# Fourteen instead of twelve column pairs per MLP multiplied with seven products, and the up projection dealt out anew between them

## The chip, the cores and the metric

The kernel runs on one core of a Trainium2 chip. The metric is the time of one execution on the device in microseconds (us); the time before is the median of three runs. The engines are named as in the profile: PE does the matmuls, DVE and ACT the elementwise work, POOL issues the accumulating DMAs, SP all other loads of weights. Each engine takes its instructions in the order in which the program holds them.

## What is computed

A trunk of two layers on 256 tokens of width 2048 in float32. Each layer adds a mixer (attention and a state space model in layer 0, dilated attention in layer 1) and then an MLP to the residual x. The change is in the MLP alone, which both layers have:

```python
def squared_relu_mlp(h, w_up, w_down):
    u = jnp.einsum('bsd,df->bsf', h, w_up)
    return jnp.einsum('bsf,fd->bsd', jnp.square(jax.nn.relu(u)), w_down)

for layer in range(DEPTH):
    h = rms_norm(x, norm_mix[layer])
    x = x + mixer(h)
    h = rms_norm(x, norm_ffn[layer])
    x = x + squared_relu_mlp(h, w_up[layer], w_down[layer])
```

w_up is 2048 x 8192 and w_down 8192 x 2048.

## The kernel before

Every product is made of three matmuls, since each float32 operand is split into a high part and a remainder (high x high, high x low, low x high). The weights are split as they come: ACT rounds a loaded piece to whi (`high`, L314), DVE subtracts it to get wlo (`low`, L324). A **piece** is two contraction tiles of 128 rows by 512 columns, 512 KB of weights.

The work is one list, `plan`, of pieces, and `run` (L291) goes through it. For piece i it records, in this order, the low part of piece i+2, the load of piece i+6, the high part of piece i+3, the sum of weights for piece i+4 (`add`, if it has one), the evictions of the piece before, then some steps of side work (`tick`), and then the piece's matmuls. So this list sets the order on all engines, and DVE and ACT work a few pieces ahead of PE, as far as the buffers go: four wraw, five whi, four wlo (L303, L320, L327).

There are two kinds of work in the list:

- A `Unit` (L227) is one stripe of 512 columns. A piece of it is 12 matmuls: two contraction tiles, two halves of 128 tokens, three matmuls each. It accumulates in two PSUM tiles `acc`. `up(i)` (L1006) makes block i (of 16) of the up projection in eight pieces; `down(c, j)` (L1012) adds chunk c's part of stripe j in four pieces. A chunk is two blocks of the up projection, 1024 rows of w_down; there are eight chunks.
- A `Seven` (L245) takes two stripes by two halves of the tokens by two blocks, that is a product of 2 x 2 with 2 x 2 blocks, and does it with seven products instead of eight. Each product has two pieces of six matmuls (tile `sp`), 14 pieces in all, in the order P1, P2, Q6, Q7, Q5, Q4, Q3. The products need sums of operands: `operands(c)` (L974) makes those of the activations on DVE, once a chunk. Sums of weight blocks are made in two ways: DVE adds them (`add`, L265: for Q6 and Q4), and POOL issues a DMA that adds a block from memory onto one that is loaded (`accumulate`, L271: after the splits of P1 and P2). Q6 needs the sum of P1's accumulated block, Q7 takes P2's accumulated block directly. The tile of all these weights is `sraw`, in a pool of 29 buffers. After each product DVE adds it into the residual `res` (`evict`, L283).

In a layer the first 16 up pieces come alone; then seven sections follow, one per chunk 0 to 6. A section lays the pieces of that chunk's sevens between a number of up pieces (`mixed`, L1036); the numbers are 20, 20, 8, 20, 20, 24 and 0 (L1049). Chunks 0, 1, 3, 4 and 5 have both of their pairs of stripes as sevens; chunk 2 has the pair 0 and 1, chunk 6 the pair 2 and 3, and their other stripes are down units. Chunk 7 is four down units, put in the last section.

Side work is held in generators that `tick` moves on, one or a few steps a piece: `squared` (relu, eight transposes `uT` on PE, squares on ACT into `uf`) and `operands` (the split of `uf` into uh and ul, then the sums s, split into sh and sl). Where a piece needs a result that the side work has not recorded yet, `need` (L189) records the steps at once. Chunk 7's `operands` waits until block 15 is squared before it splits blocks 14 and 15.

When a stripe of the residual is complete, the norm of the next layer begins on it (`Norm.begin`, L490): transposes, scaling and split into hThi and hTlo, and the sum of squares. In layer 1 the stripe is stored instead (`store`, L1118). Before, this hung on chunk 7's down unit of the stripe, which was the last to add to it.

Of the kernel before, what the change touches and what calls it, by code (L numbers as in the profile page):

```python
# [20 lines left out]
W = 512  # L21
KC = 2
NS = D // W
# [17 lines left out]
def trunk(ctx: ExitStack, tc: tile.TileContext, x, norm_mix, norm_ffn, w_up, w_down, ab_w_in, ab_q_norm,  # L41
# [107 lines left out]
    done = set()  # L149
# [95 lines left out]
    class Seven:  # L245


        def __init__(self, w, rows, c0, kts, operands, to, needs, mark):
            self.w, self.rows, self.c0, self.operands, self.to, self.needs, self.mark = \
                w, rows, c0, operands, to, needs, mark  # L250
            self.halves = kts // KC
            self.raw, self.bank = {}, {}
            self.pieces = [(self, (p, h)) for p in range(7) for h in range(self.halves)]
# [29 lines left out]
        def evict(self, p):  # L283

            name, b, _ = SEVEN[p]
            t, j, op = {"P1": (0, 0, OP.add), "P2": (0, 0, OP.add), "Q6": (1, 0, OP.add), "Q7": (1, 1, OP.subtract),
                        "Q5": (1, 1, OP.subtract), "Q4": (1, 0, OP.add), "Q3": (0, 1, OP.subtract)}[name]
            r = self.to[t][j]
            V.tensor_tensor(r, r, self.bank[b], op=op)

    def run():  # L291
        todo = plan
# [328 lines left out]
                last(t, j)  # L621
        free(ps)

    def residual_unit(w, ktiles, j, needs={}, nm=None, last=None, check=None, mark=None):
        def after(ps):
            if check is not None:
                check()
            add_stripe(ps, j, last)
            if nm is not None:
                nm.begin(j)  # L630

        return Unit([(w, j * W, W)], ktiles, after, needs=needs, mark=mark)
# [316 lines left out]
    NC = NB // 2  # L949

    def mlp(layer, nm, nxt, last=None):
        wu, wd = w_up[layer], w_down[layer]
        uf, u, sums = {}, {}, {}
# [19 lines left out]

        def operands(c):  # L974

            for k in marks[c - 1] if 0 < c < NC - 2 else [("up", layer)] if c else []:
                yield from until(k)
            if c == NC - 1:
                yield from until(("uf", layer, 2 * c + 1))
            for i in (2 * c, 2 * c + 1):  # L980
                yield from until(("uf", layer, i))
                u[i] = slot("uh"), slot("ul")
                split(u[i][0], u[i][1], uf[i])
                done.add(("u", layer, i))
# [12 lines left out]
            for (h, l), s in zip(sums[c], (s1, s2)):  # L997
                split(h, l, s)
                yield 1
# [12 lines left out]
        def down(c, j):  # L1012
            kts = [(4 * (2 * c + b) + k, (lambda b=b, k=k: u[2 * c + b] + (k,))) for b in range(2) for k in range(4)]
            marks[c].append(("down", layer, c, j))
            if c < NC - 1:
                return residual_unit(wd, kts, j, {4 * b: ("u", layer, 2 * c + b) for b in range(2)},
                                     mark=marks[c][-1]).pieces

            def whole():
                assert all(("down", layer, k, j) in done or ("down", layer, k, j - j % 2) in done for k in range(NC - 1))  # L1020

            return residual_unit(wd, kts, j, {4 * b: ("u", layer, 2 * c + b) for b in range(2)}, nxt, last, whole).pieces

        def seven(c, j):
            def parts(name):
# [5 lines left out]
            return Seven(wd, (8 * c, 8 * c + 4), j * W, 4, parts,  # L1031
                         [[res[:, t, (j + i) * W:(j + i + 1) * W] for i in range(2)] for t in range(2)],
                         {0: ("u", layer, 2 * c), 1: ("u", layer, 2 * c + 1), 2: ("sums", layer, c)},
                         marks[c][-1]).pieces

        def mixed(rest, s, start, end):  # L1036

# [8 lines left out]
        ups = sum((up(i) for i in range(NB)), [])  # L1046
        plan.extend(ups[:16])
        o = 16
        for c, n in enumerate((20, 20, 8, 20, 20, 24, 0)):  # L1049
            x, o = ups[o:o + n], o + n  # L1050
            if c == NC - 2:
                x = sum((down(c, j) for j in (0, 1)), []) + sum((down(c + 1, j) for j in range(NS)), [])
                mixed(x, seven(c, 2), 2, 19)
            elif n == 8:
                mixed(x + down(c, 2) + down(c, 3), seven(c, 0), 4.5, 16)
            else:
                mixed(x, seven(c, 0) + seven(c, 2), 4.5, n + (3 if n == 24 else 0))

    n2 = Norm(R_MIX + 16, False)
    mlp(0, n1, n2)  # L1060
# [111 lines left out]
```

## Time and profile before

| | |
|---|---|
| time, median of 3 runs (lowest to highest) | 2263.64 us (2263.55 to 2264.37) |
| the profiled execution's own time | 2264.74 us |
| its span, first to last instruction | 2262.9 us |
| DMA traffic | 475.10 MB, mean 210 GB/s |
| granted TensorE clock over the span | 1.000 |

A row of the groups reads: source line, engine, operation, output tile <- input tiles, shapes, count, then busy us and mean ns of one, then the idle time before them and what ended it. A row of the timeline or of the chain begins with the start in us from the first instruction and the duration. A row of the waits has total us, times, longest. A row of the windows has the stretch, its length, the busy us of PE, weight loads, DVE, ACT and POOL, the granted clock, the share of the DMA engines and GB/s. Nearly all instructions carry L71, the line of a helper, so tiles tell them apart: `acc` is a unit's matmul and `sp` a seven's; wlo<-wraw is the split of a unit's piece and wlo<-sraw that of a seven's.

### The profile page before, as it was taken

How to read it: one execution, taken by the hardware profiler on the slowest of the kernel's cores; microseconds unless marked ns; L12 is line 12 of the kernel's file. 1: busy time of each engine (PE TensorE's matmuls, PEld its weight loads, DVE VectorE, ACT ScalarE, POOL GpSimd, SP SyncE). 2: the span in 40 equal slices, each digit the busy share in tenths (PEclk: the TensorE clock that was granted, in tenths of full speed). 3: DMA queues.
4: the chain of work that ended last, by engine and by line, in shares of the span. 5: the costliest groups of instructions: out<-in, count | busy, mean ns of one | idle time of the engine just before them, and what ended most of it. 6: DMA issues, size and time to landing. Idle time of an engine off the chain costs nothing.

```text
span 2262.9 us, 30235 instructions
## 1 busy us (share of the span) xinstructions
PE 2247.2 (99%) x11029; PEld 1873.0 (83%) x11029; DVE 1749.7 (77%) x2482; ACT 1290.0 (57%) x1615; POOL 125.7 (6%) x116
## 2 busy tenths in 40 slices
PE   8999999999999999999999999999999999999999
PEld 7998988888888888888788778778888888888877
DVE  6779986556888888887976766665588888888786
ACT  6565545445666556565664555555566665656663
POOL 1000000000001010000000000000000000010000
PEclk9999999999999999999999999999999999999999
DMA  7546555568797797888756455546788789797874
GB/s 235 163 142 190 177 177 182 190 186 246 216 296 214 209 288 222 242 245 234 219 171 192 149 158 168 168 151 186 245 237 240 206 242 281 207 282 228 248 222 141
DMA packets 255318, 475.10 MB, mean 210 GB/s; under 512 B 17156, under 2 KB 27696, under 8 KB 255168
## 3 DMA queue, kind: packets, MB, share of 16 engines
q1 hardware_dynamic: 218976, 416.34, 56.7%
q0 software_dynamic: 26624, 50.48, 12.5%
q10 hardware_dynamic: 9568, 6.34, 0.9%
q8 instruction: 86, 1.41, 0.2%
q14 instruction: 64, 0.52, 0.1%
HBM read 470.97 MB, written 2.13 MB: 209 GB/s over the span
## 4 chain that ended last, share of the span: by engine, by line
PE 97%; DMA 1%; DVE 1%; issue 1%; ACT 0%; SPq 0%; DVEq 0%; POOLq 0%; ACTq 0%
PE acc L71 71%; PE sp L71 20%; PE uT L71 1%; PE sc L71 1%; PE o L71 1%; DMA sraw<-in_w_down_dram 1%; PE pT L71 1%; PE yp L71 1%; PE xT L71 1%; DVE wlo L71 1%; DMA wraw<-in_ab_w_in_dram 0%; PE qp L71 0%; DMA res<-in_x_dram 0%; PE yo L71 0%; PE kp L71 0%
## 5 line engine op out<-in xcount | busy, mean ns | idle before, releaser
L71 ACT ACTIVATE whi<-wraw 128x1024 fp32r<-128x1024 f32 (+1 forms) x600 | 631.9, 1054 | 493.6 <-PE acc L71 350.8
L71 DVE TENSOR_TENSOR wlo<-wraw,whi 128x1024 fp32r<-128x1024 f32 (+1 forms) x600 | 725.0, 1214 | 233.7 <-PE acc L71 159.7
L71 PE MATMUL acc<-whi,hThi 128*128 128x512 f32 (+1 forms) x1632 | 647.7, 397 | 1.8 <-ACT hThi L71 1.7
L71 PE MATMUL acc<-whi,hTlo 128*128 128x512 f32 (+1 forms) x1632 | 634.8, 389 | 1.0 <-DVE hTlo L71 1.0
L71 PE MATMUL acc<-wlo,hThi 128*128 128x512 f32 (+1 forms) x1632 | 634.1, 389 | 0.7 <-DVE wlo L71 0.7
L71 ACT ACTIVATE whi<-sraw 128x1024 fp32r<-128x1024 f32 x336 | 353.7, 1059 | 292.4 <-DVE sraw L71 137.0
L71 DVE TENSOR_TENSOR wlo<-sraw,whi 128x1024 fp32r<-128x1024 f32 x336 | 408.8, 1221 | 85.3 <-PE acc L71 35.3
L71 PEld LDWEIGHTS acc<-whi,hThi 128*128 128x128 f32 x1632 | 307.6, 188 | 66.8 <-issue 5.8
L71 PEld LDWEIGHTS acc<-whi,hTlo 128*128 128x128 f32 x1632 | 307.2, 188 | 65.7 <-DVE hTlo L71 1.8
L71 PEld LDWEIGHTS acc<-wlo,hThi 128*128 128x128 f32 x1632 | 307.9, 189 | 60.9 <-DVE wlo L71 1.1
L276 POOL DMA_DIRECT2D sraw<-in_w_down_dram x96 | 117.3, 1576 | 2058.7 <-DVE wlo L71 1815.6
L71 PE MATMUL sp<-wlo,sh 128*128 128x512 f32 x384 | 149.5, 389 | 0.0
L71 PE MATMUL sp<-whi,sl 128*128 128x512 f32 x384 | 149.5, 389 | 0.0
L71 PE MATMUL sp<-whi,sh 128*128 128x512 f32 x384 | 149.4, 389 | 0.0
L71 DVE TENSOR_TENSOR sraw<-sraw 128x1024 f32<-128x1024 f32 x96 | 117.1, 1219 | 26.4 <-DMA sraw<-in_w_down_dram 26.3
L71 DVE TENSOR_TENSOR res<-res,sp 128x512 f32<-128x512 f32 x168 | 114.7, 682 | 17.4 <-PE sp L71 17.1
L71 PE MATMUL acc<-hThi,whi 128*128 128x256 f32 x384 | 112.3, 293 | 0.0
L71 PE MATMUL sp<-whi,ul 128*128 128x512 f32 x288 | 112.1, 389 | 0.0
L71 PE MATMUL sp<-whi,uh 128*128 128x512 f32 x288 | 112.0, 389 | 0.0
L71 PE MATMUL sp<-wlo,uh 128*128 128x512 f32 x288 | 112.0, 389 | 0.0
L71 PE MATMUL acc<-hThi,wlo 128*128 128x256 f32 x384 | 108.5, 283 | 0.0
L71 PE MATMUL acc<-hTlo,whi 128*128 128x256 f32 x384 | 108.5, 283 | 0.0
(221 smaller groups left out, 2749.8 us busy)
## 6 DMA issues: line engine op xcount, KB each, us to landing
wraw<-in_w_up_dram SPq DMA_DIRECT2D x256, 512.0 KB, 5.2
sraw<-in_w_down_dram SPq DMA_DIRECT2D x192, 512.0 KB, 8.1
wraw<-in_ab_w_in_dram SPq DMA_DIRECT2D x96, 512.0 KB, 3.7
sraw<-in_w_down_dram POOLq DMA_DIRECT2D x96, 512.0 KB, 10.7
wraw<-in_c_w_qkv_dram SPq DMA_DIRECT2D x96, 512.0 KB, 4.2
wraw<-in_w_down_dram SPq DMA_DIRECT2D x64, 512.0 KB, 4.2
wraw<-in_ab_w_out_dram SPq DMA_DIRECT2D x48, 512.0 KB, 3.7
wraw<-in_c_w_o_dram SPq DMA_DIRECT2D x32, 512.0 KB, 3.6
```

The lines of the kernel that those rows point to most:

```text
L71: return f(out, *a, **k)
L276: nc.gpsimd.dma_start(self.raw[o[0], h], self.w[r * 128:(r + KC) * 128, c:c + W].rearrange("(k p) c -> p k c", p=128), accum_op=OP.add)
```

## The change

Chunks 2 and 6 take both pairs of stripes as sevens, so 14 of the 16 pairs of a layer do; only chunk 7 is left in down units. The sections' up pieces are now 18, 17, 17, 18, 17, 17 and 8: the last up unit stands in the last section, ahead of chunk 7's down units. Since a stripe's last addition may now come from chunk 6's seven or from chunk 7's down unit, a count per stripe (`early`) finds the second of the two, and the norm or the store follows that. `operands(6)` waits for chunk 5's sevens as the other chunks do for theirs, and no longer for the last up unit.

```diff
@@ class Seven
-        def __init__(self, w, rows, c0, kts, operands, to, needs, mark):
+        def __init__(self, w, rows, c0, kts, operands, to, needs, mark, after=None):
...
             V.tensor_tensor(r, r, self.bank[b], op=op)
+            if p == 6 and self.after is not None:
+                self.after()
@@ def operands(c)
-            for k in marks[c - 1] if 0 < c < NC - 2 else [("up", layer)] if c else []:
+            for k in marks[c - 1] if 0 < c < NC - 1 else [("up", layer)] if c else []:
@@ def down(c, j)
-            def whole():
-                assert all(("down", layer, k, j) in done or ("down", layer, k, j - j % 2) in done for k in range(NC - 1))
-
-            return residual_unit(wd, kts, j, {4 * b: ("u", layer, 2 * c + b) for b in range(2)}, nxt, last, whole).pieces
+            def after(ps):
+                if early[j]:
+                    add_stripe(ps, j, last)
+                else:
+                    add_stripe(ps, j)
+                early[j] += 1
+                ready(j, False)
+
+            return Unit([(wd, j * W, W)], kts, after,
+                        needs={4 * b: ("u", layer, 2 * c + b) for b in range(2)}).pieces
+
+        early = [0] * NS
+
+        def ready(j, stored=True):
+
+            if early[j] == 2:
+                if last is not None and stored:
+                    for t in range(2):
+                        last(t, j)
+                if nxt is not None:
+                    nxt.begin(j)
+
+        def sevens_end(j):
+            for k in (j, j + 1):
+                early[k] += 1
+                ready(k)
...
-                         marks[c][-1]).pieces
+                         marks[c][-1], (lambda: sevens_end(j)) if c == NC - 2 else None).pieces
@@ the list
-        for c, n in enumerate((20, 20, 8, 20, 20, 24, 0)):
+        for c, n in enumerate((18, 17, 17, 18, 17, 17, 8)):
             x, o = ups[o:o + n], o + n
+            s = seven(c, 0) + seven(c, 2)
             if c == NC - 2:
-                x = sum((down(c, j) for j in (0, 1)), []) + sum((down(c + 1, j) for j in range(NS)), [])
-                mixed(x, seven(c, 2), 2, 19)
-            elif n == 8:
-                mixed(x + down(c, 2) + down(c, 3), seven(c, 0), 4.5, 16)
+                mixed(x + sum((down(c + 1, j) for j in range(NS)), []), s, 4, 23)
             else:
-                mixed(x, seven(c, 0) + seven(c, 2), 4.5, n + (3 if n == 24 else 0))
+                mixed(x, s, 4.5, n)
```

Two places in the order of instructions are needed later. The first is DVE at the start of chunk 1's first seven in the first MLP, before the change. wlo<-sraw is the split of a seven's piece, wlo<-wraw that of an up piece, so these rows also tell in which order the pieces stand; sraw<-sraw is a sum of weights, res<-res,sp the addition of a finished product.

```order
L71 TENSOR_TENSOR wlo<-wraw,whi 128x1024
L71 TENSOR_TENSOR wlo<-sraw,whi 128x1024 x2
L71 TENSOR_TENSOR wlo<-wraw,whi 128x1024
L71 TENSOR_TENSOR sraw<-sraw 128x1024
L71 TENSOR_TENSOR wlo<-sraw,whi 128x1024
L71 TENSOR_TENSOR res<-res,sp 128x512
L71 TENSOR_TENSOR wlo<-sraw,whi 128x1024
L71 TENSOR_TENSOR sraw<-sraw 128x1024
L71 TENSOR_TENSOR wlo<-wraw,whi 128x1024
L71 TENSOR_TENSOR wlo<-sraw,whi 128x1024
```

And DVE at the same place with the change, from the split of the seven's second piece on:

```order
L71 TENSOR_TENSOR wlo<-sraw,whi 128x1024
L71 TENSOR_TENSOR wlo<-wraw,whi 128x1024
L71 TENSOR_TENSOR wlo<-sraw,whi 128x1024 x2
L71 TENSOR_TENSOR sraw<-sraw 128x1024
L71 TENSOR_TENSOR res<-res,sp 128x512
L71 TENSOR_TENSOR wlo<-wraw,whi 128x1024
L71 TENSOR_TENSOR sraw<-sraw 128x1024
L71 TENSOR_TENSOR wlo<-sraw,whi 128x1024 x2
L71 TENSOR_TENSOR res<-res,sp 128x512
L71 TENSOR_TENSOR wlo<-wraw,whi 128x1024
L71 TENSOR_TENSOR wlo<-sraw,whi 128x1024 x2
```

The seven's pieces stand in pairs with one up piece between them, where before there was an up piece after the first and then after every second; and the second sum of weights stands ahead of the split of the first sum (the first row after it), where it stood behind it.

The second place is ACT at the end of the first MLP's up projection. Before the change, at chunk 6's first down piece, the split of block 12 (uh) stands behind the weight splits (whi), with the relu of block 15 behind it:

```order
L71 ACTIVATE whi<-sraw 128x1024
L71 ACTIVATE whi<-wraw 128x1024
L71 ACTIVATE uh<-uf 128x1024
L71 ACTIVATE relu<-acc,rs_4976 128x512 x2
L71 ACTIVATE uh<-uf 128x1024
L71 ACTIVATE whi<-wraw 128x1024
```

With the change, at chunk 7's first down piece, for the splits of blocks 14 and 15:

```order
L71 ACTIVATE whi<-sraw 128x1024 x2
L71 ACTIVATE whi<-wraw 128x1024
L71 ACTIVATE relu<-acc,rs_4976 128x512 x2
L71 ACTIVATE uf<-uT 128x512 x2
L71 ACTIVATE uh<-uf 128x1024 x2
L71 ACTIVATE whi<-sraw 128x1024
```

The two relu and the two squares (uf) of block 15, with PE's eight transposes (uT) between them, now stand ahead of the split that the down piece waits for.

More of the change, by code (lines that the diff above doesn't have):

```diff
@@ L245, in trunk @@
     class Seven:
-        def __init__(self, w, rows, c0, kts, operands, to, needs, mark):
-            self.w, self.rows, self.c0, self.operands, self.to, self.needs, self.mark = \
-                w, rows, c0, operands, to, needs, mark
+        def __init__(self, w, rows, c0, kts, operands, to, needs, mark, after=None):
+            self.w, self.rows, self.c0, self.operands, self.to, self.needs, self.mark, self.after = \
+                w, rows, c0, operands, to, needs, mark, after
             self.halves = kts // KC
@@ L622, in add_stripe, with residual_unit @@
         free(ps)
-    def residual_unit(w, ktiles, j, needs={}, nm=None, last=None, check=None, mark=None):
+    def residual_unit(w, ktiles, j, needs={}, nm=None, last=None, mark=None):
         def after(ps):
-            if check is not None:
-                check()
             add_stripe(ps, j, last)
```

## The prediction, made before the changed kernel was run

> **What bounds the kernel now.** I read the page first: which engine is full, and what the chain that ended last is made of.
>
> ```profile
> PE 2247.2 (99%) x11029; PEld 1873.0 (83%) x11029; DVE 1749.7 (77%) x2482; ACT 1290.0 (57%) x1615; POOL 125.7 (6%) x116
> PE 97%; DMA 1%; DVE 1%; issue 1%; ACT 0%; SPq 0%; DVEq 0%; POOLq 0%; ACTq 0%
> ```
>
> PE is the bound: 99% busy, and 97% of the chain is PE. So a matmul that goes is time that goes, as long as PE is not made to wait. What a matmul costs on the path is not its own duration (0.39 us in the timeline, where they overlap) but the step from one to the next. The chain in order of time shows it, here in the output projection and then in the first MLP's chunk 1:
>
> ```profile
> 394.31 29.95 PE acc L71 x132
> ...
> 641.65 1.36 PE sp L71 x6
> 643.02 0.44 PE uT L71 x4
> 643.45 2.75 PE acc L71 x12
> 646.21 2.72 PE sp L71 x12
> ...
> 660.28 2.72 PE acc L71 x12
> ```
>
> 29.95 us for 132 is **0.227 us a matmul**. A piece of an ordinary unit (U below, 12 matmuls) takes 2.72 us, a piece of a seven (S, 6 matmuls) 1.36 us. I number a seven's 14 pieces S0 to S13: S0, S1 are P1, S2, S3 P2, S4, S5 Q6, S6, S7 Q7, S8, S9 Q5, S10, S11 Q4, S12, S13 Q3. Every piece, U or S, needs one split by ACT and DVE, so an S asks twice as much of DVE per microsecond of PE. How near that is to the edge shows over a whole chunk (chunk 4 of the first MLP, 20 U and 28 S), in which DVE is busy 80.94 of 94.38 us and the DMA engines 0.86:
>
> ```profile
> 881.14:975.52 94.38, 94.38 (x426) 78.16 (x424) 80.94 (x78) 57.79 (x61) 9.79 (x8) 1.00 0.86 245
> ```
>
> So in the stage that the change touches PE is the bound, but only some 13 us a chunk ahead of DVE, and DVE takes its work in order, waits included.
>
> **The change part by part.** *Products.* Two more pairs of stripes per layer (chunk 2, stripes 2 and 3; chunk 6, stripes 0 and 1) take seven products of 12 matmuls instead of eight: 12 matmuls a pair, four pairs in two layers, 48 matmuls. 48 x 0.227 = **10.9 us off the path**. What they add lies on DVE, ACT and DMA:
>
> ```profile
> L71 DVE TENSOR_TENSOR wlo<-sraw,whi 128x1024 fp32r<-128x1024 f32 x336 | 408.8, 1221 | 85.3 <-PE acc L71 35.3 <-ACT whi L71 24.6 <-issue 19.1
> L71 DVE TENSOR_TENSOR sraw<-sraw 128x1024 f32<-128x1024 f32 x96 | 117.1, 1219 | 26.4 <-DMA sraw<-in_w_down_dram 26.3
> L71 DVE TENSOR_TENSOR res<-res,sp 128x512 f32<-128x512 f32 x168 | 114.7, 682 | 17.4 <-PE sp L71 17.1
> ```
>
> Per pair six splits more (14 S for 8 U), four sums of weights, three more additions to res (7 for 4): 6 x 1.22 + 4 x 1.22 + 3 x 0.68 = 14.2 us of DVE, 57 us in all, beside PE as long as DVE has room. On the DMA queues a pair has 12 transfers instead of 8, four of them accumulating ones from POOL.
>
> *Up units dealt out anew.* This is the dear part. The chunks that had 20 U beside 28 S now have 17 or 18, and the sparse ones (chunk 2 with 16 pieces beside 14 S, chunk 5 with 24 beside 28) become like them. Around the start of a chunk's first seven the order was S0 U S1 S2 U S3 S4 U S5 S6 U S7, and becomes S0 S1 U S2 S3 U S4 S5 U S6 S7. From S0 to S4 that is the same PE work; from S4 to S7 it is one U less, so **S7 comes 2.72 us earlier**. What S7 waits for does not: its weights are made by the accumulating DMAs, which land one after the other. Chunk 1 shows all four landings, as the moments at which DVE (sums for S4, S5), then ACT (S6, S7), come off a wait for DMA:
>
> ```profile
> 646.67 1.23 DVE L71 TENSOR_TENSOR sraw<-sraw 128x1024 f32<-128x1024 f32 x1 [2.56 <-DMA sraw<-in_w_down_dram]
> 647.81 1.22 DVE L71 TENSOR_TENSOR wlo<-sraw,whi 128x1024 fp32r<-128x1024 f32 x1
> 648.95 0.68 DVE L71 TENSOR_TENSOR res<-res,sp 128x512 f32<-128x512 f32 x1
> 649.55 1.22 DVE L71 TENSOR_TENSOR wlo<-sraw,whi 128x1024 fp32r<-128x1024 f32 x1
> 650.99 1.22 DVE L71 TENSOR_TENSOR sraw<-sraw 128x1024 f32<-128x1024 f32 x1 [0.23 <-DMA sraw<-in_w_down_dram]
> ...
> 660.82 1.23 DVE L71 TENSOR_TENSOR wlo<-sraw,whi 128x1024 fp32r<-128x1024 f32 x1 [2.28 <-ACT whi L71]
> ```
>
> ```profile
> 655.09 1.06 ACT L71 ACTIVATE whi<-sraw 128x1024 fp32r<-128x1024 f32 x1 [1.71 <-DMA sraw<-in_w_down_dram]
> 659.72 2.01 ACT L71 ACTIVATE whi<-sraw 128x1024 fp32r<-128x1024 f32 x2 [2.62 <-DMA sraw<-in_w_down_dram]
> ```
>
> ```profile
> 641.49 0.39 PE L71 MATMUL sp<-whi,uh 128*128 128x512 f32 x1
> 653.32 0.39 PE L71 MATMUL sp<-whi,sh 128*128 128x512 f32 x1
> 662.84 0.39 PE L71 MATMUL sp<-whi,sh 128*128 128x512 f32 x1
> ```
>
> The last three rows are the first matmuls of S0, S4 and S7. Landings: 646.67, 650.99, 655.09, 659.72: 4.1 to 4.6 us apart. S7's split is through at 660.82 + 1.23 = 662.05, and PE reached S7 at 662.84: a spare of 0.8 us, of which the change takes 2.72. I work chunk 1 through. The second accumulating DMA is issued one piece earlier now, so at best all are 4.1 apart and the fourth lands at 646.67 + 3 x 4.1 = 658.97, 0.75 earlier; the split is through at 661.3. PE is at S7 at 662.84 - 2.72 = 660.12, its second matmul, the first that needs the low part, at 660.35: **0.95 us of waiting**. Behind it DVE has, at 1.14 us a step (647.81 to 648.95) and 0.60 for an addition to res (648.95 to 649.55): the addition, the splits of a U and of S8, a sum, S9, an addition, S10, a sum, a U. The first U's split ends at 660.07 + 1.14 + 0.60 + 1.22 = 663.0, where PE wants it by 662.6: 0.4. From 661.8 three splits and a sum (4.6), an addition (0.6), a split and a sum (2.3) put the second U's split at 669.3 to 670.5, where PE comes to it at 669.9 at the latest: 0.6. Sum: **2.0 us** in a dense first seven. Below, it could cost nothing, were the landings 2 us earlier; above, 2.75 with the landings where they are. I take 2.0: chunks 1 to 5 in two layers, 10 x 2.0 = **20 us**. The first seven of chunk 0 is dense too, but no row there waits for a DMA, and chunk 6's is thinly dealt; both at nothing. In a chunk's second seven the same U goes, but there DVE waits 0.2 us for DMA and ACT 0.9 in all:
>
> ```profile
> DVE sraw L71 <- DMA sraw<-in_w_down_dram: 0.2, 1, 0.2
> ```
>
> ```profile
> ACT whi L71 <- DMA sraw<-in_w_down_dram: 0.9, 1, 0.9
> ```
>
> I take nothing, and 1.4 each (2.72 less the 1.3 of room that the landings' spacing leaves) as the upper end.
>
> On this stands the Trainium skill, "DMA: Bandwidth & Descriptors", section "Anatomy of one DMA — SWDGE (gpsimd) path": it gives such a transfer 2.0 us and bytes at 436 GB/s, an estimate of 3.2 us for 512 KB, by which all four would have landed long before S7. The rows of the page say 10.7 us at the median against 5.2 for the plain loads beside which they run:
>
> ```profile
> wraw<-in_w_up_dram SPq DMA_DIRECT2D x256, 512.0 KB, 5.2
> sraw<-in_w_down_dram POOLq DMA_DIRECT2D x96, 512.0 KB, 10.7
> ```
>
> By that rule the 20 us would be nothing (first rival); the rows decide for the wait.
>
> *Last section of a layer.* The last up unit (15) now ends one seven piece ahead of chunk 7's first down piece, which needs the split of block 14, and that split stands on ACT and DVE behind all of block 15's squaring. Before, the nearest such place was the first down piece of chunk 6, which waited for a split only:
>
> ```profile
> PE acc L71 <- ACT uh L71: 1.5, 2, 0.7
> PE acc L71 <- DVE ul L71: 1.2, 2, 0.6
> ```
>
> ```profile
> L71 ACT ACTIVATE relu<-acc,rs 128x512 f32<-128x512 f32 x64 | 40.9, 678 | 5.0 <-PE acc L71 5.0
> L71 ACT ACTIVATE uf<-uT 128x512 f32<-128x512 f32 x64 | 37.8, 591 | 30.8 <-PE uT L71 30.7
> L71 DVE TENSOR_TENSOR ul<-uf,uh 128x1024 fp32r<-128x1024 f32 x32 | 39.1, 1223 | 18.3 <-ACT uh L71 18.3
> L71 ACT ACTIVATE uh<-uf 128x1024 fp32r<-128x1024 f32 x32 | 33.5, 1045 | 0.0
> ```
>
> That was 0.7 + 0.6 = 1.3 us a layer, and goes. New, from the end of unit 15: one weight split on ACT (1.06), two relu (1.3), at 2.5 the eight transposes (0.9 by the uT rows of the chain), two squares (to 4.4), uh (to 5.4), and 1.2 later ul. PE has S5 (1.36) and the transposes in that time, then waits 1.1 + 2.0, and 0.8 for ul: 4.0 us a layer. Below it could be 1.3 as before, above 5. Net 2 x (4.0 - 1.3) = **5.4 us**.
>
> *A stripe to the norm when both its parts are through.* Stripes 0 and 1 wait for the chunk 6 seven, which ends long before the layer; stripe 2 now comes with stripe 3 at the layer's end.
>
> ```profile
> L71 DVE SCALAR_TENSOR_TENSOR hTlo<-xT,gains,hThi 128x256 fp32r<-128x256 f32 x64 | 27.7, 478 | 15.8 <-ACT hThi L71 15.7
> L71 ACT ACTIVATE hThi<-xT,gains 128x256 fp32r<-128x256 f32 x64 | 26.0, 463 | 0.1
> ```
>
> The next unit asks for stripe 2 eight contraction tiles later, 4 x 2.72 = 10.9 us, and the stripe's steps (transposes, four of 463 ns on ACT, four of 478 on DVE) stand in the order ahead of that; cost nothing, at most the last four steps bare, 2 x 0.46 + 0.48 = 1.4. At the end of the kernel stripe 2's two stores are issued just ahead of the last stripe's:
>
> ```profile
> 2258.63 1.70 ACTq L1119 DMA_DIRECT2D out_dram<-res  x2
> ```
>
> Two issues take 1.7 us, and the last piece runs 2.7 beside them; nothing, at most 1.7. Removing the assertion costs nothing.
>
> Sum: -10.9 + 20 + 5.4 = **+14.5 us**. The profiled execution took 2264.74 us (span 2262.9), 1.1 us above the median 2263.64: 2264.7 + 14.5 - 1.1 = **2278.1 us**.
>
> **Rivals.** *Faster: the accumulating DMAs land in time.* The loads of a seven stand nearer together in SP's queue, so they could be through before POOL's first transfer instead of sharing the engines with it; decided where the fourth lands 2 us sooner. Then the 20 us are nothing: -10.9 + 5.4 = -5.5, 2258 us; with unit 15 also covered as before, 2252. For it speaks that DVE still has room on average (three U fewer take 3 x 1.14 from its 80.94 us and 8.2 from PE's 94.38: 77.5 of 86.2); against it the steady 4.1 to 4.6 us from landing to landing. *No change: only DVE's order costs.* With the landings just in time, half a microsecond a first seven is left of the U waits: 10 x 0.5 = 5, sum -0.5, 2263 us. *Worse than forecast: the second sevens wait too.* DVE comes out of a first seven without its lead; 10 x 1.0 more, 2288 us, with both upper ends 2300. That seven products save nothing isn't a rival: the order holds 48 matmuls fewer.
>
> **How the numbers follow.** Slower by the forecast's mechanism, the worse case included: 0.62, its own range 2269 to 2296. No change: 0.17. Faster: 0.21. A measurement of this kernel can tell 0.2%, 4.5 us, from no change; the cases fall on the three sides in just these shares. The range takes in most of the faster case and leaves out the far end of the worse one: 2256 to 2295.
>
> **What would show it.** Right: PE busy share below 99%; PE waiting for wlo in the order of 20 us, at Q7 pieces and the U behind them; ACT waits for DMA sraw no shorter; PE acc waits for uh and ul of 3 us a layer at the layer's end. Wrong: landings under 3.5 us apart, or PE waits that sum to under 10 us.

## The result, and the profile after

The changed kernel takes 2294.59 us (median of 4 runs, 2294.02 to 2298.45) against 2264.01 for the kernel before (2263.55 to 2265.18): ratio 1.0137, 95% interval 1.0125 to 1.0149. That is 30.6 us more where 14.5 were forecast, and 0.4 us below the upper end of the stated range. The first views of its profile, which are the engines' busy times and the chain that ended last:

```profile
PE 2257.3 (98%) x10981; PEld 1867.4 (81%) x10981; DVE 1796.2 (78%) x2534; ACT 1303.8 (57%) x1639; POOL 145.2 (6%) x132
PE 77%; DMA 12%; issue 7%; DVE 2%; ACT 1%; SPq 0%; POOL 0%; POOLq 0%; ACTq 0%; DVEq 0%
```

PE has 48 matmuls fewer, and yet it is busy 10 us longer and idle 20 us more (35.9 us of the span instead of 15.7). In the chain PE fell from 97% to 77% and DMA rose from 1% to 12%. A pause shorter than a matmul's own 0.39 us does not show as idle, so busy time alone hides half of the loss. What shows all of it is the length of a section. I cut the span at the first matmul of each seven and take from each length its matmuls at 0.2267 us and its transposes of up units at 0.118 (eight take 0.945); what is left is PE waiting. Rows of the windows of the changed kernel, first layer; the count behind PEld is matmuls and transposes together:

```profile
635.72:673.29 37.57, 37.07 (x166) 29.85 (x164) 31.64 (x30) 22.34 (x24) 4.04 (x4) 1.00 0.95 273
673.29:724.76 51.47, 50.48 (x225) 41.29 (x224) 45.42 (x45) 31.68 (x33) 5.35 (x5) 1.00 0.76 218
...
853.92:903.83 49.91, 49.91 (x226) 41.36 (x224) 44.59 (x44) 32.49 (x35) 3.64 (x4) 1.00 0.75 212
...
1085.28:1141.13 55.85, 50.85 (x217) 40.92 (x216) 42.97 (x41) 30.16 (x32) 5.27 (x5) 0.94 0.78 229
```

Chunk 1's first seven: 37.57 - 156 x 0.2267 - 0.945 = 1.26 us of waiting. Chunk 1's second seven: 1.56; chunk 3's second seven: 0.00; chunk 6's first seven (204 matmuls, 12 transposes): 8.2. In the kernel before, chunk 1's first seven (41.75 us, 180 matmuls, 8 transposes) has 0.00. Over both layers:

| us | forecast | waiting before | waiting after | change of the span |
|---|---|---|---|---|
| 48 matmuls | -10.9 | | | -10.9 |
| first sevens, chunks 1 to 5 | +20.0 | 1.3 | 18.9 | +17.6 |
| second sevens, chunks 1 to 5 | 0 | 0.0 | 11.2 | +11.2 |
| last section | +5.4 | 4.5 | 17.2 | +12.7 |
| elsewhere | 0 | | | -0.3 |
| sum | +14.5 | | | +30.3 |

The spans are 2262.9 and 2293.2, 30.3 apart, so what the table leaves over is 0.3 us. (Of the 4.5 us before, 3.8 are at chunk 6's first down piece and 0.7 at a later down piece.) Two of its rows are off the forecast: the second sevens and the last section. How a first seven waits shows in chunk 1's timeline, DVE first, then PE:

```profile
641.04 1.23 DVE L71 TENSOR_TENSOR sraw<-sraw 128x1024 f32<-128x1024 f32 x1 [2.71 <-DMA sraw<-in_w_down_dram]
642.18 0.68 DVE L71 TENSOR_TENSOR res<-res,sp 128x512 f32<-128x512 f32 x1
642.78 1.22 DVE L71 TENSOR_TENSOR wlo<-wraw,whi 128x1024 fp32r<-128x1024 f32 x1
645.03 1.23 DVE L71 TENSOR_TENSOR sraw<-sraw 128x1024 f32<-128x1024 f32 x1 [1.04 <-DMA sraw<-in_w_down_dram]
646.18 2.51 DVE L71 TENSOR_TENSOR wlo<-sraw,whi 128x1024 fp32r<-128x1024 f32 x2
```

```profile
646.69 0.39 PE L71 MATMUL sp<-whi,sh 128*128 128x512 f32 x1
647.45 0.50 PE L71 MATMUL sp<-wlo,sh 128*128 128x512 f32 x1 [0.37 <-DVE wlo L71]
...
648.71 0.40 PE L71 MATMUL sp<-whi,sh 128*128 128x512 f32 x1
```

DVE stands still for 2.71 us until the first accumulating DMA lands and for 1.04 until the second. The split for S4 stands behind the second sum, and PE, which comes to S4 at 646.69, waits for it. S5 begins at 648.71, as its own split ends (646.18 + 2.51). Over the whole kernel DVE's sums waited 26.3 us for DMA before, and now:

```profile
L71 DVE TENSOR_TENSOR sraw<-sraw 128x1024 f32<-128x1024 f32 x112 | 136.6, 1220 | 82.1 <-DMA sraw<-in_w_down_dram 82.1
```

The waits of PE; the rows of before had no seven's wait at all:

```profile
PE sp L71 <- DVE wlo L71: 7.4, 15, 0.8
PE uT L71 <- ACT relu L71: 6.1, 3, 3.1
PE acc L71 <- ACT uh L71: 3.3, 2, 1.6
```

The last two rows are the last section. Up unit 15 ends at 1103.43, and this is ACT behind it:

```profile
1105.41 1.06 ACT L71 ACTIVATE whi<-sraw 128x1024 fp32r<-128x1024 f32 x1 [2.39 <-DMA sraw<-in_w_down_dram]
1106.37 1.04 ACT L71 ACTIVATE whi<-wraw 128x1024 fp32r<-128x1024 f32 x1
1107.32 1.25 ACT L71 ACTIVATE relu<-acc,rs 128x512 f32<-128x512 f32 x2
```

Two weight splits stand ahead of the relu, and the first waits for a landing. PE is through with S5 at 1104.80 and begins chunk 7's first down piece at 1111.28. What comes then was in no view of before. Windows (granted clock in the third column from the end), then two successive matmuls of that piece:

```profile
1108.00:1111.30 3.30, 1.38 (x9) 0.90 (x9) 0.35 (x2) 2.66 (x5) 0.00 (x0) 0.71 0.00 0
1111.30:1117.00 5.70, 5.66 (x14) 4.05 (x15) 3.79 (x4) 1.98 (x3) 0.00 (x0) 0.57 0.13 28
```

```profile
1113.14 0.63 PE L71 MATMUL acc<-whi,uh 128*128 128x512 f32 x1
1113.56 0.63 PE L71 MATMUL acc<-wlo,uh 128*128 128x512 f32 x1
```

The granted clock is the mean of each window: 0.57 behind the pause, as it is 0.50 until 1116.2 and full from there on. The step from matmul to matmul is 0.42 us instead of 0.227, and the down piece takes 5.36 us instead of 2.72.

### The profile page after: what moved, and what is told of

Its sections match the earlier page's. It is cut to its first block, busy times and chain, and to the rows that moved or that the text cites. A ratio compares the mean times of both kernels' runs of the same rounds, so it can differ in the third digit from the quotient of the medians.

```text
span 2293.2 us, 30270 instructions
## 1 busy us (share of the span) xinstructions
PE 2257.3 (98%) x10981; PEld 1867.4 (81%) x10981; DVE 1796.2 (78%) x2534; ACT 1303.8 (57%) x1639; POOL 145.2 (6%) x132
## 4 chain that ended last, share of the span: by engine, by line
PE 77%; DMA 12%; issue 7%; DVE 2%; ACT 1%; SPq 0%; POOL 0%; POOLq 0%; ACTq 0%; DVEq 0%
PE acc L71 57%; PE sp L71 15%; DMA sraw<-in_w_down_dram 11%; DVE wlo L71 1%; PE sc L71 1%; PE o L71 1%; PE uT L71 1%; PE pT L71 1%; PE yp L71 1%; ACT whi L71 1%; PE xT L71 0%; DVE res L71 0%; DMA wraw<-in_ab_w_in_dram 0%; DVE sraw L71 0%; PE qp L71 0%
## 5 line engine op out<-in xcount | busy, mean ns | idle before, releaser
L71 DVE TENSOR_TENSOR wlo<-wraw,whi 128x1024 fp32r<-128x1024 f32 (+1 forms) x568 | 686.3, 1213 | 199.0 <-PE acc L71 145.4
L71 ACT ACTIVATE whi<-wraw 128x1024 fp32r<-128x1024 f32 (+1 forms) x568 | 596.7, 1052 | 416.6 <-PE acc L71 283.4
L71 ACT ACTIVATE whi<-sraw 128x1024 fp32r<-128x1024 f32 x392 | 410.9, 1058 | 396.7 <-DVE sraw L71 234.6
L71 DVE TENSOR_TENSOR wlo<-sraw,whi 128x1024 fp32r<-128x1024 f32 x392 | 474.1, 1219 | 63.8 <-ACT whi L71 34.5
L71 PEld LDWEIGHTS acc<-wlo,hThi 128*128 128x128 f32 x1632 | 308.0, 189 | 70.4 <-DVE wlo L71 11.2
L276 POOL DMA_DIRECT2D sraw<-in_w_down_dram x112 | 136.7, 1592 | 2099.3 <-DVE wlo L71 1533.3
L71 DVE TENSOR_TENSOR sraw<-sraw 128x1024 f32<-128x1024 f32 x112 | 136.6, 1220 | 82.1 <-DMA sraw<-in_w_down_dram 82.1
L71 PE MATMUL sp<-wlo,sh 128*128 128x512 f32 x448 | 177.8, 397 | 7.6 <-DVE wlo L71 7.4
L71 PE MATMUL sp<-whi,sh 128*128 128x512 f32 x448 | 175.9, 393 | 4.2 <-DVE res L71 2.8
L71 PE MATMUL sp<-whi,sl 128*128 128x512 f32 x448 | 175.4, 392 | 0.0
L71 PEld LDWEIGHTS sp<-wlo,sh 128*128 128x128 f32 x448 | 84.6, 189 | 32.5 <-DVE wlo L71 15.3
## 6 DMA issues: line engine op xcount, KB each, us to landing
sraw<-in_w_down_dram POOLq DMA_DIRECT2D x112, 512.0 KB, 10.8
```

Source lines behind the costliest of these rows:

```text
L71: return f(out, *a, **k)
L276: nc.gpsimd.dma_start(self.raw[o[0], h], self.w[r * 128:(r + KC) * 128, c:c + W].rearrange("(k p) c -> p k c", p=128), accum_op=OP.add)
```

## The experiments

Each run is compared with runs of the kernel before on the same chip (2264.0 to 2264.4). Unless said otherwise the edit is made to the changed kernel (2294.6). The waiting is worked out by sections as above, from each run's profile.

**Are the landings the cause?** The first edit leaves the accumulating transfers out, the second only their addition:

```diff
# e1
-                nc.gpsimd.dma_start(self.raw[o[0], h], ..., accum_op=OP.add)
+                return
# e6
-                                    accum_op=OP.add)
+                                    )
```

> The changed kernel without its 112 accumulating transfers; so the stripes' blocks that those would add are missing from the weights of Q6 and Q7, and of the products made from them later. Splits, sums, additions and plain loads stay. By sections, the changed kernel has 18.9 us of PE stalls in the first sevens of chunks 1 to 5 (both layers), 11.2 in their second sevens and 19.1 in chunk 6 and what lies behind it (length of a section less its matmuls at 0.227 us and its transposes at 0.118). Theory 1 (the landings of the accumulating DMAs hold PE, and in chunk 6 also hold ACT, behind whose weight split the relu of up unit 15 stands): first sevens to 0 to 2 us, second sevens to 0 to 3, chunk 6 to 9 to 12 (4 to 5 a layer for the chain relu, transposes, square, split); 2294.6 - 17 - 9 - 8 = 2260 us, range 2256 to 2266. Theory 2 (DVE has too many steps per microsecond of PE and the landings are beside the point): less than 10 us go, 2285 or more.

> The changed kernel whose 112 transfers from POOL write their block over the one in place and do not add to it, so the weights of Q6 and Q7 and of the later sums hold one block in place of a sum of two. Bytes, queues, order and waits stay. The changed kernel's accumulating transfers land 3 to 4 us apart (chunk 1: 641.02, 645.01, 648.22, 652.20), 10.8 us from issue at the median. Theory 1 (adding in place is what takes the time): landings at most 2.7 us apart, 7 us or less from issue, and the stalls of the first and second sevens (30 us) fall to under 10: 2265 to 2276 us. Theory 2 (POOL's queue of transfers beside the loads takes the time, added or not): 3.3 us apart or more, 2288 to 2297.

Measured: e1 2258.89 us (ratio 0.9976, 0.9966 to 0.9985), e6 2258.57 (0.9975, 0.9964 to 0.9986). Chunk 1's second seven and chunk 6's first seven in e1:

```profile
672.61:722.52 49.91, 49.91 (x225) 41.33 (x224) 45.80 (x45) 32.26 (x33) 0.00 (x0) 1.00 0.54 178
1067.85:1120.90 53.05, 50.23 (x217) 40.56 (x216) 42.98 (x41) 30.38 (x32) 0.00 (x0) 0.97 0.62 206
```

Every first and second seven of chunks 1 to 5 waits 0.00 us in both runs; chunk 6 keeps 5.4 a layer in e1. DVE, with the same steps in the same order, makes no wait there by itself. And with the addition gone, the same bytes on the same queue land sooner; POOL's transfers and DVE's sums in e6:

```profile
sraw<-in_w_down_dram POOLq DMA_DIRECT2D x112, 512.0 KB, 6.9
```

```profile
L71 DVE TENSOR_TENSOR sraw<-sraw 128x1024 f32<-128x1024 f32 x112 | 136.6, 1220 | 10.4 <-DMA sraw<-in_w_down_dram 9.9
```

6.9 us from issue against 10.8 with addition, and 2.1 us from one landing of a seven to the next against 3.7 (medians). Theory 1 holds in both, in e6 by more than it said: the time is 6.4 us below its range (2265 to 2276), since no stall is left in chunks 1 to 5.

**Where does the lost unit tell?** e2 puts it back between S0 and S7; e4 gives chunks 1 and 2 the even pattern of chunk 3:

```diff
# e2
-                mixed(x, s, 4.5, n)
+                mixed(x, s, 5, n + 0.3)
# e4
-        for c, n in enumerate((18, 17, 17, 18, 17, 17, 8)):
+        for c, n in enumerate((16, 18, 18, 18, 17, 17, 8)):
```

> The changed kernel with the sevens of chunks 0 to 5 dealt half a unit later: S0 U S1 S2 U S3 S4 U S5 S6 U S7 again, as in the kernel before; the same work. Theory 1 (the fourth landing comes too late for an S7 that PE reaches one up unit early): the first sevens' 18.9 us fall to 2 to 6; the second sevens, whose pattern changes but stays as dense, keep 8 to 14; chunk 6 as it is: 2294.6 - 15 = 2280 us, range 2275 to 2284. Theory 2 (too many DVE steps, wherever S7 stands): the stalls come at other pieces, 2291 to 2298.

Measured: 2278.54 us (2276.27 to 2281.01). First sevens 6.2 us, second sevens 8.4, chunk 6 as before. As theory 1 has it.

> The changed kernel with 16, 18, 18, 18, 17, 17, 8 up units in the sections: chunks 1 and 2 are dealt as chunk 3 is (an up unit behind every two seven pieces, no three seven pieces in a row); chunk 0 gets denser, chunks 3 to 6 stay. Theory 1 (the second sevens stall where three seven pieces stand in a row, S8 S9 S10 and S3 S4 S5, because the missing up unit leaves DVE no time to get its lead back; chunk 3's second seven stalls 0.0 us): second sevens of chunks 1 and 2 from 1.57, 1.18, 1.60, 1.60 us to 0.0 to 0.3 each, 5 to 6 us in all; chunk 0 up by 0 to 3; 2294.6 - 4.5 = 2290 us, range 2287 to 2293. Theory 2 (a second seven stalls because the first one took DVE's lead, whatever the pattern): these four stay at 1 us or more, 2293 to 2297.

Measured: 2294.33 us (2291.4 to 2296.28), the time that theory 2 named; the sections say theory 1. Chunks 1 and 2, second sevens, first layer:

```profile
674.89:724.80 49.91, 49.91 (x226) 41.33 (x224) 45.24 (x44) 31.34 (x33) 3.19 (x4) 1.00 0.76 219
764.95:814.90 49.95, 49.95 (x226) 41.33 (x224) 44.91 (x44) 32.59 (x35) 3.05 (x4) 1.00 0.75 214
```

All four wait 0.00 to 0.04 us, where they waited 5.95 together. The gain was given back elsewhere: chunk 1's first seven waited 4.7 us in one layer, for a unit's wlo (2.8 in one wait). On DVE that split stands behind the splits of the sums s, these wait for ACT, and ACT waited 4.5 us for a plain load of up weights; that this comes of the denser chunk 0 is not shown.

e4 changed two things in the second sevens at once. In the changed kernel those of chunks 1, 2, 4 and 5 have the row S3 S4 S5 without a unit, and they also have a unit between S0 and S1. POOL's transfers wait for the splits of the first pieces, so they go out later against PE. Here is chunk 1 of the first layer before, where S0 starts at 683.24, and then in the changed kernel, where it starts at 673.29:

```profile
679.66 4.91 POOL L276 DMA_DIRECT2D sraw<-in_w_down_dram  x4 [34.06 <-DMA wraw<-in_w_up_dram]
```

```profile
671.10 1.20 POOL L276 DMA_DIRECT2D sraw<-in_w_down_dram  x1 [32.54 <-DVE wlo L71]
673.49 3.68 POOL L276 DMA_DIRECT2D sraw<-in_w_down_dram  x3 [1.18 <-DVE wlo L71]
```

The first landing comes 5.4 to 6.9 us behind the start of S0 in those four chunks. It came 2.1 to 2.9 us behind it in chunks 1, 3 and 4 before, and comes 2.2 to 3.2 in e4's chunks 1 and 2. The traces say that it takes both, the row and the late landing. Without late landings the same row costs nothing (e1, e6). And in e2's chunk 3 the first landing comes 7.0 and 5.8 us behind S0, but no three pieces stand in a row up to S5, and the second seven waits 0.2 and 0.0 us.

**Is it DVE's order?** e5 moves the sums behind the split and one piece later:

```diff
                 low(i + AHEAD - 1)
                 fetch(i + AHEAD - 1 + RAW)
+                add(i + AHEAD)
                 high(i + AHEAD)
-                add(i + AHEAD + 1)
```

> The changed kernel in which DVE forms a seven piece's sum of weights three pieces ahead and behind that step's split, not four ahead and in front of it: the split for S4 no longer stands behind the sum for S5, which waits for the second landing. Same work. Theory 1 (what binds is the chain from a landing: in the first sevens of chunks 1 to 4 PE begins S5 3.70 us after the second landing, whatever stands ahead, so a wait taken from S4 comes back at S5): 2294.6 less 0 to 4, 2290 to 2295 us. Theory 2 (DVE's order makes the stalls, S4's split being held by a sum that nobody needs yet): S4's 0.6 to 1.0 us go in nearly every seven and DVE is ahead again behind them, 10 us or more, 2278 to 2285.

Measured: 2353.0 us, 58 more: neither theory. DVE's splits now wait for ACT (34.5 us in the changed kernel), and ACT for DVE's sums:

```profile
L71 DVE TENSOR_TENSOR wlo<-sraw,whi 128x1024 fp32r<-128x1024 f32 x392 | 473.7, 1222 | 164.8 <-ACT whi L71 142.7 <-issue 15.4 <-PE acc L71 3.5
```

The sum's early place is the lead itself: later, sum, rounding and split of each piece go one after the other between two engines that wait for each other. So this run does not test what it was made for.

**The last section.** e3 splits block 14 as soon as it is squared (`halves(i)` is the part of `operands` that splits block i, and chunk 7's `operands` no longer waits for block 15 first); e11 adds two seven pieces ahead of block 15's first reader; e12 also places unit 15's steps when they are due:

```diff
# e3, and e11 and e12
         def after_up(i, ps):
             side(squared(i, ps), ("uf", layer, i))
+            if i == NB - 2:
+                side(halves(i))
...
# e11 and e12
-                mixed(x + sum((down(c + 1, j) for j in range(NS)), []), s, 4, 23)
+                d = sum((down(c + 1, j) for j in range(NS)), [])
+                mixed(x + d[:2], s[:8], 4, 9.5)
+                plan.extend(s[8:11])
+                mixed(d[2:], s[11:], 1, 13.3)
# e12 (`urgent` holds the squaring of block 15 and the operands of chunk 7)
...
     def tick(heavy=False):
         clock[0] += 1
+        for t in list(tasks):
+            if t[2] in urgent and t[0] <= clock[0]:
+                step(skip=[o for o in tasks if o is not t])
```

> The changed kernel in which block 14 is split as soon as its own unit is squared, and only block 15 is left to be split after the last up unit (its first reader is two down pieces and several seven pieces later). Theory 1 (chunk 6's 19.1 us are the chain from the last up unit to block 14's split, with the relu held on ACT behind a weight split that waits for a landing, and matmuls that run at half speed after the pause): chunk 6 falls to 2 to 6 us, 2294.6 - 15 = 2280 us, range 2276 to 2284. Theory 2 (PE would wait there for the landing of its own seven piece in any case): 6 us or less go, 2288 or more.

> The changed kernel, with its accumulating DMAs, block 14 split early as in the run before (2286.8), and S9 and S10 of chunk 6's first seven dealt between chunk 7's second and third down piece, so that block 15's first reader comes 2.7 us later. Theory 1 (what was left there, 4.2 us a layer, is block 15's own chain late by 1.8 + 0.5 us and the matmuls at half speed behind that pause): 2286.8 - 8 = 2279 us, range 2275 to 2282. Theory 2 (a landing is what was late): 2284 or more.

> As in the run with room for block 15 (2287.6 us), and the steps of up unit 15's squaring and of the two last splits are placed when they are due, not held back until a reader asks for them (the builder holds side steps back while its count of DVE work is above 1200; there it placed block 15's square and split only at chunk 7's third down piece). Theory 1 (the 4.2 to 5.4 us a layer that stayed there are this late placing, and the half-speed matmuls behind the pause that it makes): chunk 6's first half to 0 to 2 us a layer, 2287.6 - 8 = 2280 us, range 2276 to 2283. Theory 2 (unit 15's chain is too long for any place there): 2285 or more.

Measured: e3 2286.84 us, e11 2287.64, e12 2283.52 (2280.02 to 2287.33). Waiting in chunk 6's first seven, by layer: 8.2 and 9.1 in the changed kernel, 4.3 and 4.2 in e3, 5.4 and 4.6 in e11, 1.5 and 1.2 in e12. e3 missed its range (2276 to 2284): it brought half the gain. e11's room did nothing; its time is the one named for a late landing, but ACT in e11 shows another reason: the relu of unit 15 is done by 1107.3, and then

```profile
1117.58 0.57 ACT L71 ACTIVATE uf<-uT 128x512 f32<-128x512 f32 x1
1118.19 1.06 ACT L71 ACTIVATE uh<-uf 128x1024 fp32r<-128x1024 f32 x1
```

The second square comes ten microseconds behind the relu, with chunk 7's third down piece; in e3 that piece came sooner, and so did the square (1113.89). The step follows its reader, because the builder holds side work back while its count of DVE work is high and places it when a reader asks. Placed when due (e12), the stall goes, though the median time is 0.5 us above the range named for that (2276 to 2283); the profile is that of its fastest run. Chunk 6's first seven, first layer, at full clock:

```profile
1083.17:1132.30 49.13, 48.13 (x218) 39.35 (x216) 42.35 (x41) 29.57 (x32) 7.37 (x7) 1.00 0.85 256
```

**A mend by dealing alone.** e7 has 18 up units in chunks 0 to 5 and 4 in chunk 6, S0 ahead of its unit and block 14 early; e8 adds e5's edit, and with e5's finding it tells nothing more (2363.8 us).

```diff
-        for c, n in enumerate((18, 17, 17, 18, 17, 17, 8)):
+        for c, n in enumerate((18, 18, 18, 18, 18, 18, 4)):
...
-                mixed(x + sum((down(c + 1, j) for j in range(NS)), []), s, 4, 23)
+                mixed(x + sum((down(c + 1, j) for j in range(NS)), []), s, 0, 18)
             else:
-                mixed(x, s, 4.5, n)
+                mixed(x, s, 5, n + 0.3)
```

> Fourteen pairs with seven products, dealt anew: 18 up units in each of chunks 0 to 5 and 4 in chunk 6, each seven's S0 before the unit that it stood behind (S0 U S1 S2 U S3 S4 U S5 S6 U S7), block 14 split as soon as it is squared, and in chunk 6 one seven piece more between the last up unit and chunk 7's second down piece. If the ledger holds (stalls are where a landing, or block 14 and 15, is late, and nowhere else): first sevens from 18.9 us to 3 to 8, second sevens from 11.2 to 0 to 3 (chunk 3's in the run with the sevenths later: 0.2 and 0.0), chunk 6 from 19.1 to 3 to 9: 2294.6 - 35 = 2260 us, range 2253 to 2267. If new waits take their place: 2270 or more.

> The same with the sums of weights three pieces ahead and behind that step's split. Theory 1 (a landing's own chain binds, not DVE's order): within 3 us of the run without it. Theory 2 (DVE's order): 4 us or more below it.

Measured: e7 2287.12 us (five runs from 2284.0 to 2295.7), a miss by 27. First sevens fell to 8.8 us, second sevens of chunks 1 to 4 to 1.8, but a new wait took their place: without the four units between chunk 5's S13 and chunk 6's S0, chunk 6 starts before its activations are split (chunk 6's first seven 10.8 and 10.6 us):

```profile
PE sp L71 <- DVE ul L71: 3.7, 2, 1.9
...
PE sp L71 <- ACT sh L71: 2.8, 2, 1.4
```

**Another maker for the sums.** e9 lets POOL's adder make all four sums of a seven in place of the DMAs (e10 with e3's edit beside it); e13 lets DVE make the first of the four, e14 the first two:

```diff
# e9
-                nc.gpsimd.dma_start(self.raw[o[0], h], ..., accum_op=OP.add)
...
+            nc.gpsimd.tensor_tensor(u.raw[a, h], u.raw[a, h], u.raw[b, h], op=OP.add)
# e13; e14 with BY_DVE = (0, 1)
+    BY_DVE = (0,)
...
+            if p == 1 and h in BY_DVE:
+                V.tensor_tensor(self.raw["11", h], self.raw["11", h], self.raw["12", h], op=OP.add)
-            if o is not None:
+            if o is not None and not (p == 0 and h in BY_DVE):
```

> The changed kernel without its accumulating DMAs: both blocks of each of those sums are in SBUF as plain loads anyway, so POOL's own adder forms them (112 additions of 128x1024), as soon as the split that reads the old value is through and the second block is there. Theory 1 (the landings make all stalls in chunks 1 to 5): if POOL takes 2.5 us or less for one (DVE: 1.22), all of the first and second sevens' stalls go, chunk 6 keeps the 5.4 a layer that stayed without the accumulating transfers: 2259 us, range 2255 to 2264. Theory 2 (any maker of these sums off DVE is late, or POOL slows DVE down): POOL at 4 us or more for one or DVE's split above 1.3 us, 2280 or more.

> The same with block 14 split as soon as it is squared. Without a landing on ACT the relu of up unit 15 goes at once and block 15 is ready in time for its first reader, so the 5.4 us a layer go as well: 2248 us, range 2245 to 2253, below both kernels. If block 15 is still late: 2254 or more.

Measured: e9 2407.99 us, e10 2406.22, far above the 2259 and 2248 of the first theory. Theory 2 named the reason, a split on DVE above 1.3 us: it takes 1.48 at the mean, and PE waits 98.8 us for wlo. POOL's additions, DVE's splits, and two of these on DVE's timeline:

```profile
L295 POOL TENSOR_TENSOR sraw<-sraw 128x1024 f32<-128x1024 f32 x112 | 351.9, 3162 | 2003.5 <-DVE wlo L71 1913.0 <-ACT whi L71 51.0 <-DVE s L71 37.2
L71 DVE TENSOR_TENSOR wlo<-sraw,whi 128x1024 fp32r<-128x1024 f32 x392 | 575.6, 1483 | 39.6 <-issue 30.3 <-ACT whi L71 1.9 <-PE acc L71 1.8
```

```profile
649.52 6.74 DVE L71 TENSOR_TENSOR wlo<-sraw,whi 128x1024 fp32r<-128x1024 f32 x2
```

> The changed kernel in which DVE, not an accumulating DMA, makes the first of a seven's four sums in place (both blocks are in SBUF by then): 28 accumulating DMAs fewer, 28 DVE steps of 1.14 us more. The three others stay and should land 2 to 4 us sooner. Theory 1 (the chain of landings makes the stalls in chunks 1 to 5, DVE has room): first sevens from 18.9 us to 2 to 8, second sevens from 11.2 to 0 to 3, chunk 6 a little less than 19: 2294.6 - 25 = 2269 us, range 2260 to 2275. Theory 2 (DVE has no room left for these 32 us): 2285 or more.

> The same with the first two of the four sums made by DVE: 56 DVE steps of 1.14 us more (64 us), two accumulating DMAs left in a seven. Theory 1: no landing is late any more in chunks 1 to 5, first and second sevens 0 to 3 us in all, chunk 6 5 to 8 a layer: 2262 us, range 2257 to 2267. Theory 2 (DVE, at 77.5 + 4.6 us of 86 in a chunk and in order, becomes what is waited for): 2272 or more.

Measured: e13 2265.93 us (ratio 1.0007, 0.9998 to 1.0016), e14 2266.82 (1.0012, 1.0003 to 1.0021). In e13 all first and second sevens of chunks 1 to 5 together wait 1.6 us instead of 30.1, chunk 0 0.9 a layer, chunk 6 7.3 and 6.3. DVE's sums in e13, 28 more than in the changed kernel:

```profile
L71 DVE TENSOR_TENSOR sraw<-sraw 128x1024 f32<-128x1024 f32 x140 | 170.5, 1218 | 20.3 <-DMA sraw<-in_w_down_dram 20.3
```

So to take one landing out of the chain of four is enough, though the three that are left still land 4.0 us apart at the median, and DVE has room for 32 us more. With two, DVE begins to be late (chunk 0 waits 2.0 a layer).

**Both causes taken away.** e15 is e13 and e12 in one kernel.

> Both mends at once: DVE makes the first of a seven's four sums, and block 14 is split early, block 15's steps are placed when due, with the 2.7 us of room. If the two are all there is to the loss and do not touch each other: the run with DVE's one sum (2265.9, chunk 6's first half 7.3 and 6.3 us) less the 11 us that the other mend takes from there: 2255 us, range 2251 to 2259, below the kernel before. If the last section's stall comes back with DVE's added steps: 2261 or more.

Measured: 2253.11 us (2252.33 to 2254.96), ratio 0.9953 (0.9939 to 0.9967): 0.5% below the kernel before, 41.5 us below the changed one. The two causes add up nearly: e13 and e12 took 28.7 and 11.1 us off the changed kernel, 39.7 together. The waiting in chunks 0 to 6 is 4.2 us in all. Its engines:

```profile
PE 2235.5 (99%) x10981; PEld 1863.6 (83%) x10981; DVE 1825.2 (81%) x2562; ACT 1303.8 (58%) x1639; POOL 110.5 (5%) x104
```

## Why the prediction had the side right and the size wrong

- **Products, -10.9 us: right.** e15, which also keeps all fourteen pairs, waits 4.2 us in chunks 0 to 6 where the kernel before waits 5.8; its profiled span is 12.1 us below (2250.8 against 2262.9), 10.9 for the matmuls and the rest about what the waits make.
- **First sevens, +20: right in cause (e1, e13), and close in size, 17.6 measured, in part by luck.** Of the 18.9 us, 13.3 lie where the working put 19.5: S7 6.7 (9.5 in the working), the unit behind it 3.0 (4), the unit behind S10 3.6 (6). The other 5.6 lie where it had none: S4 and the unit ahead of it 4.2, the unit behind S5 1.4. There the sums for S4 and S5 hold DVE until the first and second landing. The working followed the chain from the fourth landing on and left out what the first three already did to DVE's lead.
- **Second sevens, "I take nothing": this step failed**, by 11.2 us. It reasoned that DVE waited only 0.2 us for a landing there before. But that row was read with the old dealing: a unit between any two pairs of pieces, and the first landing 2.8 us behind the start of S0. With 17 units a first seven has the row S8 S9 S10 without one and a second seven the row S3 S4 S5, and in the second sevens of chunks 1, 2, 4 and 5 the first landing comes 5.4 to 6.9 us behind S0. They then wait (chunk 5's in the second layer hardly), chunk 3's, with 18 units, do not. e4 took both the row and the late landing away from chunks 1 and 2, and 5.95 us became 0.03. Of the 11.2 us, 10.2 are PE waiting at S4, whose split stands behind S5's sum, which waits for the second landing, as in the first sevens. The text's own upper end, 1.4 each, is what chunks 1 and 2 show (1.2 to 1.6). Chunk 4's show 0.8 and 0.2, chunk 5's 4.1 and 0.0. Of the 4.1, some 1.4 are seven matmuls at a step of 0.43 us, behind the first waits, where the granted clock was 0.50 for 3.4 us.
- **Last section, +5.4: mis-sized, 12.7 measured.** 4.0 us a layer were taken for block 14's chain, with one weight split ahead of the relu. The trace has two, one of them waiting for a landing that the same prediction made late elsewhere; relu began 3.9 us behind the unit, not 1.1. The pause was 5.5 us of PE outside the transposes, not 3.1, and the down piece behind it lost 2.6 us, not 0.8, at a granted clock of 0.50, which no quoted row of before had shown. The runs split the cause: 5.4 us a layer stay without landings (e1), 1.2 to 1.5 with block 14 split early, the room and the steps placed when due (e12). The old wait that was taken off, 1.3 us a layer, is 1.9 by sections. The order had shown where these steps stand; it was read for what stood ahead of the split, not for what held it back.
- **Rest, 0: right.** The norm's and the stores' new places make no more than 0.3 us with all else.
- **The rivals.** That DVE's order alone costs (no change) is refuted by e1: no landing, no wait. That landings come in time (faster) did not happen, but e6 and e13 show that it would have decided as the text said: in e13 a first seven's last landing comes 14.7 us behind the start of S0 instead of 16.9 (medians), the 2 us that the text named as the deciding point, and the sevens cost next to nothing (though DVE makes one of the sums there). The rival "second sevens wait too", with 10 x 1.0 us and 2288, is what happened, together with the larger last section. The estimate of 3.2 us for a transfer by the Trainium skill, "DMA: Bandwidth & Descriptors", section "Anatomy of one DMA — SWDGE (gpsimd) path", was not met, neither with addition (10.8) nor without (6.9).
- **The signs.** PE's share fell below 99% (98), ACT's rounding of a seven's pieces waited longer for landings (55.2 us instead of 41.1), and the landings stood 3.7 us apart. But the view of PE's waits has 9.6 us for wlo (7.4 and 2.2), where 20 were looked for: most of the stops are shorter than a matmul and do not show there. The wait for uh was 1.6 us a layer and not 3; the rest of that pause stands as a wait for the relu.

## What to carry to other kernels

Where a dense schedule replaces a sparse one, price each repeated place by what stood between its instructions before, not by the wait that it showed: a wait of zero says only that there was cover. Ask as well what the new order does to the moment at which a transfer is issued. Follow an in-order engine from its first late input on, since all behind it is late with it. And compare by sections: one run here (e4) had the time of one theory and the sections of the other.

## What the runs showed of the hardware that was not expected

- A 512 KB transfer that adds to what it finds in SBUF landed 10.8 us from issue at the median, the same transfer without addition 6.9 (e6); 3.7 and 2.1 us from one landing of a seven to the next.
- POOL's addition of 128x1024 took 3.16 us at the mean (2.39 the shortest), and a DVE step beside it 3.4 instead of 1.22 (two in 6.74 us), so POOL's idle time was not free to use (e9). The Trainium skill, "Advanced Engine Details and Errata", section "GPSIMD Details", says that POOL conflicts with DVE instructions that have two inputs in SBUF; this run agrees, and 112 such additions made the kernel 113 us slower (2408.0 against 2294.6).
- Around a pause of PE of some 5 us the granted clock was 0.50, for 6.8 us in the first layer and 10.2 in the second, and a matmul's step 0.42 us instead of 0.227. In chunk 5's second seven (first layer) two gaps of 1.4 and 0.6 us, with one matmul between them, were enough for 3.4 us at 0.50. The Trainium skill, "TensorE: Matmul & The Clock Gate", section "Part 1: The HAM clock gate", gives half the clock behind an idle window of some 3.4 us and 426.7 ns for a matmul of 512 columns then; the clock and the step agree, though chunk 5's two gaps are shorter than that window. A pause of this length cost its own time and some 2 us more here.
